# A decoder step's first stage: rope and splitting straight from PSUM, and a weighted sum moved to TensorE

## The chip, the cores and the metric

The kernel runs on one core of a Trainium2 chip. Its engines work side by side, each through its own instruction stream in order: TensorE (PE, with its weight loads shown as PEld), VectorE (DVE), ScalarE (ACT), GpSimd (POOL), and SyncE (SP), whose queue starts nearly all DMA transfers here. The metric is the device time of one execution in microseconds; lower is better. A single run is compared by the median of several executions.

## The reference, cut to what matters

One inference step of a one-layer decoder. 2048 prompt tokens and 32 sample tokens (8 sequences of 4 new tokens) are normed and projected; half of the columns feed a windowed attention of 8 heads of 64, the other half an mLSTM. What matters here is the projection of the attention half, and the sample tokens' attention over a cache of 2048 keys and values per sequence:

```
u = rmsnorm(x) @ w_in;  qa, ka, va, za = columns of u
qa, ka = rope(qa), rope(ka)        # only the first 16 of each head's 64 columns turn:
                                   # x1*cos - x2*sin, x2*cos + x1*sin with x1, x2 = 8 columns each
new_k, new_v = ka, va              # outputs, in float32
# sample tokens, three patterns (window 128, 512, 2048; every key, every 4th, every 16th):
s = einsum('bthe,btjhe->bthj', q, kg) * 64**-0.5
p = exp(s - max);  acc = einsum('bthj,btjhe->bthe', p, vg)   # then merged over the patterns
```

## The kernel before, in words

The program has three stages: `phase_a` (projection, sample attention), `phase_b` (prompt attention), `phase_c` (mLSTM and output). The change is all in `phase_a`. A planner decides the order of the instructions on every engine from its own model of times, except where the program fixes it; then each engine executes its list strictly in order.

`phase_a` first loads the five 1024 x 512 weight blocks (q, k, v and two gates z). Each is scaled by its largest value (`weight_scale`, which needs a `partition_all_reduce` on POOL, L87) and split into a high and a low float16 part, high on ACT, low on DVE (L105) or POOL (L102 and L103). Then it goes over the 16 tiles of 128 prompt tokens. `unit(i, j)` is one tile times one weight block: 24 float16 products of 128 x 128 by 128 x 512 (L143 to L145) into one PSUM bank of four (`ps_proj`, tag "proj").

For q, k and v the unit goes on so: ACT copies the bank to SBUF as float32 `u`, of which there are two buffers (L463); for q and k DVE turns the first 16 columns of every head in `u` with four instructions (L198 to L201); ACT writes the high float16 part to `t16` (L469); POOL subtracts to get the low part (L470); for k ACT copies the high part once more (L472); for v DVE writes two constant columns into `t16` (L474, L475); SP stores `t16` (L476); for k and v POOL scales `u` into `kvout` (L479) and SP stores that to the output (L480). `t16` has one buffer for each of q, k and v, and `kvout` one. For z, ACT copies the bank and SP stores it (L459, L460).

While tiles 4 to 9 run, the loop also prepares six more weight blocks (loaded by L72, written out by L128 from `wst`), and calls `SampleAttention.scores(b)` for the eight sequences: POOL multiplies cached keys by the query (L332), DVE sums (L337). `softmax` follows in tile 9. In tiles 10 to 14 `values(b)` runs for each sequence: for the patterns 2, 1, 0 the cached values (128 keys x 4 tokens x 512, or 128 x 512 shared by the four tokens for pattern 0) are loaded (L317, L321); POOL multiplies patterns 2 and 1 by the probabilities (L382), DVE pattern 0 (L387, four instructions), DVE adds the three (L392, two instructions), and TensorE sums over the keys by one float32 product per token (L395), 32 in all, whose stationary operand is a column of ones in a window of `oh`. The bank `ps_dec` collects all 32 rows. `finish` then divides and stores. The gate units of the last three tiles come after that, and the first products of `phase_b` follow.

Of the kernel before, what the change touches and what calls it, by code (L numbers as in the profile page):

```python
# [10 lines left out]
F32 = mybir.dt.float32  # L11
# [38 lines left out]
def in_order(G, *engines):  # L50
    """Keeps what the block traces on each of these engines in the order of the trace; yields what comes last on each."""
# [14 lines left out]
def weight_loads(G, pool, src, n, tags=("wf", "wf")):  # L66
    """The two halves of src [128, KT, n] (DRAM)."""
# [13 lines left out]
def weight_scale(G, mx, inv, g, rowscale=1.0 / XSC):  # L81
    """The scale of each kt, and inv to undo it, from the four parts' maxima."""
# [25 lines left out]
def weights(G, pool, inv, wf, n, g=None, rowscale=1.0 / XSC, sb=None, dst=None, use=None, shared=0):  # L108
    """wf (of weight_loads) times g, scaled to 2^14 at most, as two float16 parts [128, 2, KT, n], in sb or (DRAM) dst;
    inv undoes the scales. use(j, t) sees the halves t [128, 2, KT / 2, n] that go to dst."""  # L110
# [22 lines left out]
def token_matmuls(nc, ps, x16, tok, hi, lo, cols):  # L133
    """ps[token, col] = x16[:, hi|lo, kt, tok]^T @ (hi|lo)[:, kt, cols], three float16 products."""
    for _ in token_steps(nc, ps, x16, tok, hi, lo, cols):
        pass
# [12 lines left out]
def add_eighths(eng, sq, other):  # L149
    """sq[:, 0] <- the sum of all of sq and other, [128, 4, n] each."""  # L150
# [5 lines left out]
def norm_factors(G, ps, sq, n, tag="", eng=None):  # L156
    """From the squares' sums sq[:, 0] [128, n] the columns' factors, on all partitions: ps[:, 256:256 + n]."""
# [12 lines left out]
def norm_columns(G, pool, pp, xf, x16, n, other, tag="", eng=None):  # L170
    """x16 [128, 2, KT, n] <- rmsnorm (no gain) of the columns of xf [128, KT, n], times XSC, as two float16 parts."""
# [16 lines left out]
def as_f32(x16):  # L188
    """The memory of x16's second part, as [128, 4, 256] float32."""
    return x16[:, 1].rearrange("p k t -> p (k t)").bitcast(F32).rearrange("p (k t) -> p k t", k=4)  # L190


def rope(nc, pool, u, rc, rs, n):
    """u [n, heads, 64] in place; rc, rs [n, 16]."""
# [9 lines left out]
def sample_matmuls(nc, ps, xd, hi, lo, cols):  # L204
    """ps[hi | lo rows of the sample tokens, col]: the two halves are added by the caller."""
# [6 lines left out]
def sample_sum(G, pool, out, ps, sc, n, tag="dhalf"):  # L212
    """out [32, n] = sc * (ps[0:32] + ps[32:64])."""
# [9 lines left out]
def bulk(G, n, after):  # L223
    """The next n pieces of the caches' copies, issued behind an instruction of GpSimd's."""
# [6 lines left out]
class SampleAttention:  # L231
    """Attention of the sample tokens over the cache and the new rows, in steps that the caller spreads out."""

    def __init__(self, G, I, O, pool, pp):
# [5 lines left out]
        self.oh = t("d_oh", [P, 2 * NS])  # L240
        nc.gpsimd.memset(self.oh, 0.0)
        nc.gpsimd.memset(self.oh[:, NS - 1:NS], 1.0)
# [9 lines left out]
    def project(self, j, hi, lo):  # L252
        """j: q, k, v, attention gate, mLSTM gate."""
# [1412 lines left out]
```

## Time and profile before

| | us |
|---|---|
| three runs | 1835.0 (median), 1827.64, 7943.17 |
| span of the profiled execution | 1837.1 |
| PE busy in that span | 1514.6 (82%) |
| DVE busy | 1213.3 (66%) |
| POOL busy | 679.0 (37%) |
| ACT busy | 637.9 (35%) |

The runs' times are those of whole executions; the profile gives for its execution the span from the first to the last instruction and no other time. The profiled span is 2.1 us, or 0.1%, above the median of the runs. Busy time counts an engine's instructions from start to end, and idle time says nothing by itself: what counts is who waits for whom.

### The profile page before, as it was taken

Reading aid. Unit: us, or ns where it says so; the run is one execution under the profiler, and the core shown is the slowest. Engines: PE = TensorE matmul, PEld = TensorE weight load, DVE = VectorE, ACT = ScalarE, POOL = GpSimd, SP = SyncE. Lnnn points to the kernel's source line nnn. Section 1 sums busy time; section 2 is a strip of 40 time slices with the busy share of each in tenths; the row PEclk is TensorE's granted clock in tenths of the full one; section 3 lists DMA queues with packets and bytes.
Section 4 is the critical chain, followed back from the end, with each engine's and each line's share of the span. In section 5 each row is a group of like instructions: output and inputs, shape, how many; then the busy total and the mean of one; then the engine's idle time right before and its main releaser. Section 6 shows DMA issues by size and latency. Waiting matters only on the chain.

```text
span 1837.1 us, 27998 instructions
## 1 busy us (share of the span) xinstructions
PE 1514.6 (82%) x10303; PEld 898.6 (49%) x10303; DVE 1213.3 (66%) x3177; ACT 637.9 (35%) x1330; POOL 679.0 (37%) x836
## 2 busy tenths in 40 slices
PE   2847479777778668999999999688969979898987
PEld 1313234333333222477777886455545545565643
DVE  4541377666677999476766675577668666767765
ACT  2232123123232111276656675233223323232332
POOL 2343045353454788063433677211122212122210
PEclk9978789888979789899989999889989989999998
DMA  5421447676675456396655665635454434446413
GB/s 174 148 93 53 155 142 257 227 274 219 220 245 170 140 162 222 115 333 201 171 201 154 230 217 179 188 99 180 132 159 140 161 128 160 149 163 199 106 41 63
DMA packets 165927, 311.08 MB, mean 169 GB/s; under 512 B 12109, under 2 KB 117742, under 8 KB 155726
## 3 DMA queue, kind: packets, MB, share of 16 engines
q1 hardware_dynamic: 161694, 230.29, 40.9%
q0 software_dynamic: 3952, 78.75, 11.3%
q8 instruction: 81, 1.33, 0.3%
q14 instruction: 56, 0.46, 0.1%
q10 hardware_dynamic: 144, 0.26, 0.0%
HBM read 232.00 MB, written 144.38 MB: 205 GB/s over the span
## 4 chain that ended last, share of the span: by engine, by line
PE 28%; DVE 16%; DMA 10%; issue 4%; ACT 4%; POOL 1%; SPq 0%; POOLq 0%; ACTq 0%; DVEq 0%
DMA Mb<-g_scr 4%; PE ps_s L999 4%; PE ps_t L1021 4%; PE ps_s L1000 4%; DMA A<-att_scr 4%; DVE cd L1156 3%; DVE d_vb L387 2%; PE ps_out L145 2%; PE ps_out L143 2%; PE ps_out L144 2%; PE ps_k L666 1%; PE ps_o L1037 1%; PE ps_o L1038 1%; PE ps_o L1039 1%; PE ps_qk L1140 1%
## 5 line engine op out<-in xcount | busy, mean ns | idle before, releaser
L143 PE MATMUL ps_proj<-wa,x 128*128 128x512 f16 x640 | 253.4, 398 | 37.5 <-ACT u L463 22.6
L144 PE MATMUL ps_proj<-wa,x 128*128 128x512 f16 x640 | 252.8, 397 | 19.4 <-POOL wa L103 19.2
L145 PE MATMUL ps_proj<-wa,x 128*128 128x512 f16 x640 | 252.5, 395 | 0.0
L1008 DVE CUSTOM_DVE_ANT_0 sc<-ps_s,mask,ncqk 128x256 f32<-128x256 f32 (+1 forms) x384 | 144.2, 422 | 53.2 <-PE ps_s L1000 41.8
L1010 POOL TENSOR_SCALAR sc<-sc,o 128x256 f32<-128x256 f32 (+1 forms) x272 | 114.0, 431 | 153.5 <-DVE o L1008 145.1
L144 PEld LDWEIGHTS <-x 128*128 128x128 f16 x768 | 74.6, 100 | 111.8 <-issue 44.8
L1025 DVE SCALAR_TENSOR_TENSOR tl<-ps_t,th 128x512 f16<-128x512 f32 (+1 forms) x152 | 103.1, 681 | 36.5 <-ACT th L1024 35.6
L145 PEld LDWEIGHTS <-x 128*128 128x128 f16 x768 | 75.1, 101 | 104.4 <-issue 36.8
L143 PEld LDWEIGHTS <-x 128*128 128x128 f16 x768 | 75.4, 101 | 103.0 <-issue 27.3
L1024 ACT ACTIVATE th<-ps_t 128x512 f16<-128x512 f32 (+1 forms) x152 | 89.8, 591 | 80.1 <-PE ps_t L1021 78.0
L470 POOL TENSOR_TENSOR t<-u,t 128x512 f16<-128x512 f32 x48 | 67.0, 1397 | 119.1 <-ACT t L469 59.6
L469 ACT ACTIVATE t<-u 128x512 f16<-128x512 f32 x48 | 30.1, 629 | 211.0 <-DVE u L201 107.1
L1021 PE MATMUL ps_t<-c_id,pr 128*128 128x128 f32 x600 | 100.3, 289 | 1.4 <-DVE tl L1025 1.2
L143 PE MATMUL ps_out<-wo,yt 128*128 128x512 f16 x256 | 101.2, 395 | 0.0
L144 PE MATMUL ps_out<-wo,yt 128*128 128x512 f16 x256 | 101.0, 394 | 0.0
L1140 PE MATMUL ps_qk<-cx,wb 128*128 128x256 f16 x256 | 75.1, 293 | 31.0 <-ACT pre L1149 20.7
L145 PE MATMUL ps_out<-wo,yt 128*128 128x512 f16 x256 | 97.3, 390 | 2.9 <-DVE yt L1251 2.9
L1323 POOL TENSOR_TENSOR qi<-qi,qk 128x128 f32<-128x128 f32 x60 | 27.8, 494 | 189.2 <-DMA qi<-g_scr 175.6
L1140 PE MATMUL ps_qk<-early_x,wb 128*128 128x256 f16 x256 | 72.6, 284 | 22.9 <-ACT pre L1149 17.5
L1141 PEld LDWEIGHTS <-wb 128*128 128x128 f16 x512 | 52.8, 103 | 65.2 <-issue 56.2
L1156 DVE SCALAR_TENSOR_TENSOR cd<-pre,cw,cd 128x256 f32<-128x256 f32 x168 | 84.1, 505 | 0.6
L1037 PE MATMUL ps_o<-v,th 128*128 128x65 f16 x600 | 80.4, 196 | 1.5 <-ACT th L1024 1.0
(461 smaller groups left out, 4245.9 us busy)
## 6 DMA issues: line engine op xcount, KB each, us to landing
s_win_k<-cache_win_k POOLq DMA_DIRECT2D x32, 1022.0 KB, 9.3
s_win_v<-cache_win_v POOLq DMA_DIRECT2D x32, 1022.0 KB, 8.0
wf<-w_in SPq DMA_DIRECT2D x18, 1024.0 KB
d_kv<-cache_win_k SPq DMA_DIRECT2D x16, 1024.0 KB
d_kv<-cache_win_v SPq DMA_DIRECT2D x16, 1024.0 KB
A<-att_scr SPq DMA_DIRECT2D x16, 792.0 KB
v<-v_scr SPq DMA_DIRECT2D x12, 1040.0 KB
w_scr<-wst SPq DMA_DIRECT2D x12, 1024.0 KB
```

The costliest lines, as they stand in the source:

```text
L143: nc.tensor.matmul(ps, lhsT=xh, rhs=hi[:, kt, cols], start=kt == 0, stop=False)
L144: nc.tensor.matmul(ps, lhsT=xh, rhs=lo[:, kt, cols], start=False, stop=False)
L145: nc.tensor.matmul(ps, lhsT=xl, rhs=hi[:, kt, cols], start=False, stop=kt == KT - 1)
L999: nc.tensor.matmul(o, lhsT=q, rhs=k[0], start=True, stop=False)
L1008: nc.vector.tensor_tensor_reduce(sc[:, x:x + n], sp[:, x:x + n], G.mask[:, 2 * P - n:], G.ncqk, BIG, ALU.add, ALU.min, nm)
L1010: nc.gpsimd.tensor_scalar(sc[:, x:x + n], sc[:, x:x + n], -1.0, nm, ALU.mult, ALU.add)
L1021: nc.tensor.transpose(out=tp[:, c * P:(c + 1) * P], in_=pr[:, c * P:(c + 1) * P], identity=G.idf)
L1024: nc.scalar.activation(th[:, :w], tp[:, :w], AF.Copy, scale=PSC)
L1025: nc.vector.scalar_tensor_tensor(tl[:, :w], tp[:, :w], PSC, th[:, :w], ALU.mult, ALU.subtract)
L1037: nc.tensor.matmul(o, lhsT=th[:, cs], rhs=V[:, 0:65], start=first, stop=False)
L1140: nc.tensor.matmul(ps, lhsT=hi[:, kt, cols], rhs=x16[:, 0, kt], start=kt == 0, stop=False)
L1156: eng.scalar_tensor_tensor(d, pre[:, j:j + 256], cw[:, ct, j:j + 1], d, ALU.mult, ALU.add)
```

## The change

In `unit`, `u` goes away: ACT and DVE read the PSUM bank directly. The rope table is scaled by 2^-19 on the host, so that its products need no scaling. For q and k DVE forms the two products of rope from the bank (`ra`, and `rb` in one instruction that reads the two halves of 8 columns in reversed order), adds them into a small tile `r`; ACT writes the high part of columns 16 to 63 of every head, and for k and v the scaled float32 output `o`, both from the bank; DVE forms the low part from the bank and the high part with one instruction. POOL only copies and subtracts the 16 turned columns (128 columns in all), and for k scales them into `o`. For v nothing is left on POOL. `t16` of q and k now shares three buffers; v has two of its own, whose constant columns are set once; `o` has two.

In `values` the multiplication by probabilities and the sum over keys become one float32 product per pattern and token: its stationary operand is the 128 x 32 block of probabilities (4 tokens x 8 heads) and its moving operand the 128 x 512 values. The four tokens' products go to four different groups of 32 partitions of one bank (tag "den", one buffer) and accumulate over the three patterns. DVE then keeps of every row the head that belongs to it (a mask), and one more float32 product with a 0/1 matrix adds the 128 rows into the 32 rows of `ps_dec`. Mask and matrix come in one small constant, `c_dsel`, by a DMA that takes the place of two memsets on POOL.

```diff
-        self.oh = t("d_oh", [P, 2 * NS])
-        nc.gpsimd.memset(self.oh, 0.0)
-        nc.gpsimd.memset(self.oh[:, NS - 1:NS], 1.0)
+        self.sel = t("d_sel", [P, HA + 2 * NS - NTOK])
+        nc.sync.dma_start(out=self.sel, in_=I["c_dsel"])
...
-        acc = None
+        ps = self.pp.tile([P, 512], F32, tag="den", name="ps_dv", bufs=1)
         for a in (2, 1, 0):
-            p = self.sc[:, a, b].rearrange("p t h -> p (t h)").unsqueeze(2).broadcast_to([P, NTOK * HA, DA])
             t = self.piece("cache_win_v", b, a, ("wst", "wf", "d_kv")[a])
-            tv = t.rearrange("p t (h d) -> p (t h) d", d=DA)
-            if a:
-                nc.gpsimd.tensor_tensor(tv, tv, p, ALU.mult)
-            else:
-                u = self.pool.tile([P, NTOK, 512], F32, tag="d_qb", name="d_vb")
-                for i in range(NTOK):
-                    pi = self.sc[:, 0, b, i].unsqueeze(2).broadcast_to([P, HA, DA])
-                    nc.vector.tensor_tensor(u[:, i].rearrange("p (h d) -> p h d", d=DA), t[:, 0].rearrange("p (h d) -> p h d", d=DA), pi, ALU.mult)
-                t = u
-            if acc is None:
-                acc = t
-            else:
-                nc.vector.tensor_tensor(acc, acc, t, ALU.add)
-        for i in range(NTOK):
-            r = b * NTOK + i
-            nc.tensor.matmul(self.ps_o[:NS], lhsT=self.oh[:, NS - 1 - r:2 * NS - 1 - r], rhs=acc[:, i], start=r == 0, stop=r == NS - 1)
+            p = self.sc[:, a, b].rearrange("p t h -> p (t h)")
+            for i in range(NTOK):
+                nc.tensor.matmul(ps[i * 32:(i + 1) * 32], lhsT=p, rhs=t[:, i if a else 0], start=a == 2, stop=a == 0)
+        u = self.pool.tile([P, HA, DA], F32, tag="d_z", name="d_vs")
+        nc.vector.tensor_tensor(u, ps.rearrange("p (h d) -> p h d", d=DA), self.sel[:, 0:HA].unsqueeze(2).broadcast_to([P, HA, DA]), ALU.mult)
+        c0 = HA + NS - NTOK - b * NTOK
+        nc.tensor.matmul(self.ps_o[:NS], lhsT=self.sel[:, c0:c0 + NS], rhs=u.rearrange("p h d -> p (h d)"), start=b == 0, stop=b == NB - 1)
...
+        v16 = [pool.tile([P, HA, 130], F16, tag=f"v16{j}", name="v16") for j in range(2)]
+        for t in v16:
+            nc.gpsimd.memset(t[:, :, 64:65], 1.0)
+            nc.gpsimd.memset(t[:, :, 65:66], 0.0)
...
-            u = pool.tile([P, 512], F32, tag="u", name="u", bufs=2)
-            nc.scalar.activation(u, ps, AF.Copy, scale=USC)
-            uh = u.rearrange("p (h d) -> p h d", d=DA)
+            pv = ps.rearrange("p (h d) -> p h d", d=DA)
+            R = 0 if j == 2 else 16
+            t16 = v16[i % 2] if j == 2 else pool.tile([P, HA, (2 * DA, 3 * DA)[j]], F16, tag="t16", name="t16", bufs=3)
+            l0 = 66 if j == 2 else DA
+            o = pool.tile([P, HA, DA], F32, tag="kvout", name="kvout", bufs=2) if j else None
             if j < 2:
-                rope(nc, pool, uh, G.rope_p[:, i, 0:16], G.rope_p[:, i, 16:32], P)
-            w, l0, scr = ((2 * DA, DA, G.q_scr), (3 * DA, DA, G.k_scr), (130, 66, G.v_scr))[j]
-            t16 = pool.tile([P, HA, w], F16, tag=f"t16{j}", name="t16")
-            nc.scalar.activation(t16[:, :, 0:DA], uh, AF.Copy)
-            nc.gpsimd.tensor_tensor(t16[:, :, l0:l0 + DA], uh, t16[:, :, 0:DA], ALU.subtract)
+                ra = pool.tile([P, HA, 16], F32, tag="ra", name="ra")
+                rb = pool.tile([P, HA, 16], F32, tag="rb", name="rb")
+                r = pool.tile([P, HA, 16], F32, tag="rr", name="rr", bufs=2)
+                table = lambda c, n: G.rope_p[:, i, c:c + n].unsqueeze(1).broadcast_to([P, HA, n])
+                nc.vector.tensor_tensor(ra, pv[:, :, 0:16], table(0, 16), ALU.mult)
+                two = lambda x: x.rearrange("p h (a e) -> p h a e", a=2)
+                nc.vector.tensor_tensor(two(rb), two(pv[:, :, 0:16])[:, :, ::-1], two(table(16, 16)), ALU.mult)
+            nc.scalar.activation(t16[:, :, R:DA], pv[:, :, R:], AF.Copy, scale=USC)
+            if j:
+                nc.scalar.activation(o[:, :, R:], pv[:, :, R:], AF.Copy, scale=G.wainv[:, j:j + 1])
+            nc.vector.scalar_tensor_tensor(t16[:, :, l0 + R:l0 + DA], pv[:, :, R:], USC, t16[:, :, R:DA], ALU.mult, ALU.subtract)
+            if j < 2:
+                nc.vector.tensor_tensor(r, ra, rb, ALU.add)
+                nc.gpsimd.tensor_copy(t16[:, :, 0:16], r)
+                nc.gpsimd.tensor_tensor(t16[:, :, DA:DA + 16], r, t16[:, :, 0:16], ALU.subtract)
             if j == 1:
+                nc.gpsimd.tensor_scalar(o[:, :, 0:16], r, G.isc[:, 1:2], 0.0, ALU.mult, ALU.add)
                 nc.scalar.activation(t16[:, :, 2 * DA:], t16[:, :, 0:DA], AF.Copy)
-            elif j == 2:
-                nc.vector.memset(t16[:, :, 64:65], 1.0)
-                nc.vector.memset(t16[:, :, 65:66], 0.0)
...
-                nc.gpsimd.tensor_scalar(o, u, G.isc[:, j:j + 1], 0.0, ALU.mult, ALU.add)
```

## Rows read from the trace of the kernel before

**Rows 1.** The stages: busy us of each engine, granted clock, DMA share, GB/s.

```profile
0.00:196.00 196.00, 117.15 (x520) 51.17 (x521) 79.77 (x189) 54.75 (x94) 67.86 (x100) 0.90 0.40 127
196.00:300.00 104.00, 70.70 (x372) 32.95 (x372) 63.20 (x96) 26.20 (x37) 36.59 (x17) 0.84 0.48 153
300.00:590.00 290.00, 232.01 (x1137) 103.35 (x1135) 197.01 (x259) 79.96 (x122) 129.63 (x64) 0.89 0.69 234
590.00:736.00 146.00, 100.27 (x442) 37.74 (x443) 137.57 (x103) 20.26 (x34) 115.81 (x40) 0.84 0.53 170
```

**Rows 2.** PE's waits from 0 to 300: who, us in total, times, longest.

```profile
PE ps_proj L143 <- ACT u L463: 18.7, 3, 9.3
...
PE ps_ss L162 <- DVE sq L153: 29.6, 2, 20.2
PE ps_proj L143 <- ACT z L459: 4.2, 1, 4.2
```

**Rows 3.** What ACT's copy of the bank (L463) waited for; POOL's all-reduce.

```profile
  POOL t L470: 52.1, 14
...
L87 POOLq MODIFY_POOL_CONFIG  x24: 1/11/37, 24.6 to 496.5; - x24
```

**Rows 4.** POOL, SP, DVE and PE around 210, in order of time.

```profile
204.23 1.11 POOL L470 TENSOR_TENSOR t<-u,t 128x512 f16<-128x512 f32 x1 [7.45 <-issue]
...
208.98 0.07 DVE L474 MEMSET t<- 128x8 f16 x1 [8.49 <-DMA v_scr<-t]
210.45 0.59 SPq L72 DMA_DIRECT2D wf<-w_in  x1
218.60 2.35 DVE L78 TENSOR_REDUCE wmx<-wf 128x1 f32<-128x1024 f32 x2 [8.59 <-DMA wf<-w_in]
223.32 1.01 PE L162 MATMUL ps_ss<-ones,sq 128*128 128x1 f32 x4 [20.23 <-DVE sq L153]
```

**Rows 5.** POOL's groups from 300 to 600; SP's longest waits from 0 to 800.

```profile
L470 POOL TENSOR_TENSOR t<-u,t 128x512 f16<-128x512 f32 x22 | 26.0, 1180 | 66.6 <-ACT t L469 36.6 <-issue 23.2 <-ACT x L176 6.9
L479 POOL TENSOR_SCALAR kvout<-u,isc 128x512 f32<-128x512 f32 x14 | 12.1, 861 | 24.6 <-DVE u L201 14.9 <-DVE t L475 7.7 <-issue 2.0
...
SPq L476 <- POOL t L470: 164.8, 35, 17.8
SPq L480 <- POOL kvout L479: 82.5, 21, 17.3
```

**Rows 6.** Groups of the values' stretch, 590 to 736: busy us, mean ns, idle before.

```profile
L382 POOL TENSOR_TENSOR d_kv<-d_kv,d_sc 128x2048 f32<-128x2048 f32 x16 | 64.2, 4025 | 7.0 <-DMA d_kv<-cache_win_v 6.2 <-ACT d_sc L352 0.8
L387 DVE TENSOR_TENSOR d_vb<-d_kv,d_sc 128x512 f32<-128x512 f32 x32 | 60.6, 1949 | 0.0
L395 PE MATMUL ps_dec<-d_kv,d_oh 128*32 128x512 f32 x56 | 30.9, 704 | 20.8 <-DVE d_kv L392 20.8
L392 DVE TENSOR_TENSOR d_kv<-d_kv 128x2048 f32<-128x2048 f32 x8 | 20.1, 2514 | 0.0
```

**Rows 7.** DVE instructions by line: ns min/median/max, first and last start.

```profile
L198 DVE TENSOR_TENSOR ra<-u,rope_p x32: 272/291/4406, 52.8 to 714.2; 128x128 f32<-128x128 f32 x32
L1025 DVE SCALAR_TENSOR_TENSOR tl<-ps_t,th x152: 543/689/693, 780.8 to 1129.7; 128x512 f16<-128x512 f32 x144, 128x384 f16<-128x384 f32 x8
L404 DVE TENSOR_TENSOR d_rep<-d_rep,ps_dec x1: 650/650/650, 745.4 to 745.4; 32x512 f32<-32x512 f32 x1
```

**Rows 8.** Weight loads of the values' float32 products (two for each product), in order.

```profile
738.29 0.18 PEld L395 LDWEIGHTS ps_dec<-d_kv,d_oh 128*32 128x32 f32 x1 [0.68 <-issue]
...
740.74 0.11 PEld L395 LDWEIGHTS ps_dec<-d_kv,d_oh 128*32 128x32 f32 x1 [0.32 <-issue]
```

**Rows 9.** POOL and ACT instructions nearest to the new ones; waits for DVE's rope.

```profile
L841 POOL COPY dT<-dT 128x192 f32<-128x192 f32 x1 | 0.4, 393 | 0.0
L857 POOL TENSOR_TENSOR dT<-dT 128x128 f32<-128x128 f32 x1 | 0.5, 460 | 0.0
...
  ACT t L469: 107.1, 13
```

More of the change, by code (lines that the diff above doesn't have):

```diff
@@ L471, in unit @@
             if j == 1:
+                nc.gpsimd.tensor_scalar(o[:, :, 0:16], r, G.isc[:, 1:2], 0.0, ALU.mult, ALU.add)
                 nc.scalar.activation(t16[:, :, 2 * DA:], t16[:, :, 0:DA], AF.Copy)
-            elif j == 2:
-                nc.vector.memset(t16[:, :, 64:65], 1.0)
-                nc.vector.memset(t16[:, :, 65:66], 0.0)
+            scr = (G.q_scr, G.k_scr, G.v_scr)[j]
             nc.sync.dma_start(out=scr.rearrange("r t e -> t r e")[rows], in_=t16.rearrange("p (r h) e -> p r (h e)", r=4))
@@ L477, in unit @@
             if j:
-                o = pool.tile([P, 512], F32, tag="kvout", name="kvout")
-                nc.gpsimd.tensor_scalar(o, u, G.isc[:, j:j + 1], 0.0, ALU.mult, ALU.add)
-                nc.sync.dma_start(out=O["p_win_k" if j == 1 else "p_win_v"][rows, :], in_=o)
+                nc.sync.dma_start(out=O["p_win_k" if j == 1 else "p_win_v"][rows, :], in_=o.rearrange("p h d -> p (h d)"))
         def gate_unit(i):
@@ L1575, in constants @@
 def constants():
-    rp = _rope_table(np.arange(S)).reshape(NT, P, 32).transpose(1, 0, 2)
+    rp = _rope_table(np.arange(S)).reshape(NT, P, 32).transpose(1, 0, 2) * np.float32(USC)
     t = np.arange(P)
@@ L1583, in constants @@
     dmask = np.where(key < np.arange(NTOK)[None, :], -BIG, 0.0).astype(np.float32)
+    i, i2, h = np.arange(P) // 32, np.arange(P) // HA % NTOK, np.arange(P) % HA
+    keep = (i == i2)[:, None] & (h[:, None] == np.arange(HA)[None, :])
+    dsel = np.concatenate([keep, np.arange(2 * NS - NTOK)[None, :] == (NS - NTOK + i)[:, None]], axis=1).astype(np.float32)
     r = np.arange(NS)
@@ L1590, in constants @@
     rs = _rope_table(16384 + r % NTOK)
-    return {"c_dmask": dmask, "c_d32": d32, "c_block": block, "c_rope_s": rs, "c_causal": causal, "c_rope_p": rp, "c_mask": mask, "c_id": np.eye(P, dtype=np.float32)}
+    return {"c_dsel": dsel, "c_dmask": dmask, "c_d32": d32, "c_block": block, "c_rope_s": rs, "c_causal": causal, "c_rope_p": rp, "c_mask": mask, "c_id": np.eye(P, dtype=np.float32)}
 def host_layout(a):
```

## The prediction, made before the change was run

> **What bounds the kernel now.** I first read the stages [rows 1]. Up to 736 us no engine is full for long: PE is busy 117.2 of 196 us, 70.7 of 104, 232.0 of 290 and 100.3 of 146. After 770 the kernel is a different one, and the change touches nothing there. So the question is what makes PE wait in the first 770 us, and that has a different answer in each stretch. In the views of waits one looks for what the waiting instruction waited for, and then for what that one waited for, until an engine is reached that was really working.
>
> Before 300 us the waits [rows 2] name ACT's copy of the bank (18.7 us), ACT's copy of a gate (4.2 us) and a DVE sum (29.6 us, of which 20.2 in one piece). ACT's copy in turn mostly waited for POOL's subtraction L470, 52.1 us over the program [rows 3]: there are two buffers `u`, and POOL gives them back. POOL is not busy but it stands still: each of the twelve all-reduces L87 comes with two changes of its configuration (24 in rows 3), and around one of them one sees the first ordinary instruction behind a gap of 7.45 us [rows 4]. Whatever is queued on POOL pays for these gaps.
>
> From 300 to 590 PE is ahead of everything else, and the slow thing is the chain load, largest value, all-reduce, split, store of each weight block, beside the scores, on POOL, DVE and SP. SP issues in order and waits 164.8 us for L470's results and 82.5 us for `kvout`, and the loads behind these wait with them [rows 5].
>
> From 590 to 736 DVE is the bound: 137.6 of 146 us [rows 1]. Of that L387 is 60.6 us and L392 20.1 us twice (the row shown and its twin, 40 us), together 101 us; POOL's L382 is another 64.2 us, and PE waits 20.8 us for the sum [rows 6]. Much of L387 is not work: its mean is 1949 ns, while the rope instruction L198, also from SBUF and SBUF, takes 291 ns in the median and 4406 at most [rows 7]; the long ones lie beside POOL's long multiplications.
>
> **The change part by part.** *Evacuation, 0 to 196 us.* What goes: PE's 18.7 us behind `u` and 4.2 us behind the gate [rows 2], 22.9 us in all, since a bank no longer needs a buffer that POOL gives back. What is next: the weight blocks still come at the pace of POOL's all-reduces, which stay with their gaps, and this pace may eat all of it. Bounds 0 and 22.9 us; I take 10, a little under half, because in this stretch PE's work already waits for weights as well.
>
> *The constant columns, 196 to 223 us.* Here one can follow a chain by eye [rows 4]: POOL comes late to L470 (204.23, after its gap), v's tile is stored after it, DVE's memset L474 waits for that store because v has a single buffer (8.49 us), behind it on DVE stands the last split of a weight, behind that the load of the next weights (210.45), and PE finally stands still until 223.32. The memsets leave the loop and v has two buffers, so DVE's 8.49 us go. I take 8.5, bounds 0 and 8.5: the load must then still land.
>
> *POOL in the loop, 300 to 590 us.* Out go L470 and L479, 26.0 and 12.1 us [rows 5], that is 38.1 us for 22 units, 7.3 tiles. In come, per tile, for q a copy and a subtraction of 128 columns, bounded by 393 and 460 ns [rows 9], 0.85 us; for k the same and one scaling, at most 0.39 us more, 1.24 us; for v nothing. 7.3 x 2.1 = 15 us. POOL saves 23 us; with SP's queue less often behind POOL I take 12 as what reaches the end, bounds 0 (DVE, or a transfer, is late instead) and 23.
>
> What DVE and ACT get: DVE loses two of its eight rope instructions per tile and the memsets, and gets three low parts, priced by L1025 (bank and SBUF, 543 ns for 384 columns at least, 689 for 512): 0.54 + 0.54 + 0.69 = 1.8 us per tile. Against that, only the sum `ra + rb` still reads two SBUF tiles. L1025 works from a bank while POOL is also busy, and never took more than 693 ns in 152 [rows 7], so I cost DVE at nothing net; if DVE is on the path there, it is up to 7.3 x 1.8 = 13 us, which lies inside the bounds above. ACT's waits for DVE's rope (107.1 us, [rows 9]) lose their reason, but a new one stands in their place: k's second copy now waits for POOL's copy of 16 columns, and behind it on ACT are the next banks and the weights' high parts. ACT stood at the same place before, for DVE, so I add nothing for this. A bank is now held until DVE has read it too; with four banks PE may run four units ahead.
>
> *The values, 590 to 736 us.* DVE loses 101 us and gets eight maskings of a bank at 650 ns (L404, [rows 7]), 5 us. It falls to 137.6 - 101 + 5 = 42 us, POOL loses 64.2 us. Next late is PE or the transfers. PE now has 100.3 us of which 30.9 are L395, so 69.4 of other work. The new float32 products are 8 x (12 + 1) = 104 where 32 were. One product is two weight loads and two passes, and a pass takes 0.11 + 0.32 = 0.43 us late in the group and 0.18 + 0.68 = 0.86 us early [rows 8], that is at the 2.4 and at the 1.2 GHz level; PE had waited before the early ones. No row shows products to four different groups of 32 partitions, so their overlap is bounded from both sides. None: 104 x 0.86 = 89 us at 2.4 GHz. Full, four for one: 8 x (3 + 1) x 0.86 = 27.5 us. I take the value between them that follows from order: PE takes instructions in order, the two passes of one product use the same columns and must follow each other, but the second pass of one can run beside the first of the next. Four products then take five passes, and the stretch 8 x (3 x 5 x 0.43 + 0.86) = 58 us. PE's sum is 69.4 + 58 = 127.5 us against 146: 18.5 us gained. Each sequence's products also wait for DVE to have masked the bank of the one before (one buffer), 0.65 us, with other units to put between. The transfers: 170 GB/s over 146 us are 24.8 MB [rows 1]; at the 234 GB/s of the stretch before they need 106 us, so they bound the gain at 40.
>
> The Trainium skill speaks to this term (TensorEngine Tiling (Array Packing), Key Properties): different tiles of the array run their loads and products in parallel, and changing the tiling drains the engine. No row of this trace shows the first; by it all four products would run at once, and the third rival below is what that gives. The second speaks against the change, since the units' 128-column products stand between; L395 already mixes 32-column products with them, so the old kernel pays it too.
>
> *The small constant* is one transfer for two memsets on POOL at the first stage's start, and hidden there.
>
> The sum: 10 + 8.5 + 12 + 18.5 = 49 us. The profiled span is 0.1% above the median of the runs, so it comes off the median: 1835 - 49 = 1786 us.
>
> **The rivals.** *Products one after the other.* If groups of 32 columns don't overlap at all, and at the mean of this trace (30.9 us for 28 products, 1.10 us each), the 104 take 115 us and PE 184 us, 38 more than the stretch has now. 1835 - 30.5 + 38 = 1843 us. For it: no row shows an overlap. Against: PE is ahead of the stretch when it begins and could have done more of the units earlier.
>
> *Products at the 1.2 GHz level: the slower side.* The products now wait in PE's order for each loaded piece, 24 of them, with the units queued behind. If PE stands still before each as it did before L395, the products begin at the lower level: 104 x 2 x 0.86 = 179 us without overlap, PE 248 us, 102 more than now: 1835 - 30.5 + 102 = 1907 us. It decides once a product costs PE more than (146 + 30.5 - 69.4) / 104 = 1.03 us, and is slower by over 2% from 1.4 us. For it: the early loads of rows 8 and the granted clock of 0.84 in that stretch, one of the two lowest. Against: fewer engines have to meet before a product can start.
>
> *Full overlap.* PE needs 69.4 + 27.5 = 97 us, the transfers 106: gain 40 us, 1835 - 30.5 - 40 = 1764 us. For it: the groups share no columns. Against: the two passes of each product.
>
> *The change doesn't reach the path:* POOL's gaps and the loads hold the first 590 us as before, and only the values' 18.5 us come: 1816 us. For it: 0.40 to 0.69 DMA share and the all-reduces stay. Against: the chain of rows 4 and SP's waits both start at what is removed.
>
> **How the numbers follow.** Forecast 1786 us (own range 1762 to 1812): 0.42. Full overlap: 0.18. One after the other: 0.17. Not on the path: 0.10. The lower level: 0.13. Below every bound: 22.9 + 8.5 + 23 + 40 = 94 us gain, 1741 us. The range 1741 to 1843 leaves out the slower rival and little else. A measurement of this kernel tells about 2% from no change, so faster is below 1798 us: 0.18 and three quarters of 0.42 and a few of the others, 0.53. Slower, above 1872 us: 0.13 and a little for an order that the planner gets wrong, 0.15. The rest, 0.32, is the same.
>
> **What would show it.** Right: no waits of PE on ACT's copy; DVE's waits for v's store gone and the 20 us gap before 223 halved; SP's waits for POOL's results under a third; DVE below half in the values' stretch, and that stretch 15 to 40 us shorter; the second product of a group starting before the first ends. Wrong: PE waiting for DVE to free a bank, ACT waiting for POOL's copy for tens of us, the values' products in a row at 0.86 us each with the units late behind them, or a first stage that ends where it did, with the loads as the reason.

## The result, and the profile after

The changed kernel takes 1744.2 us (median) beside 1828.5 us for the kernel before; the ratio is 0.953 with a 95% interval of 0.949 to 0.957. It is faster by 84 us where 49 were forecast. Executions more than 1.5% above the fastest of their kernel, such as the one of 7943 us before, are left out of all medians and ratios.

Both programs can be cut at the same four points, and the first rows to read are those that place them. This is one line of each kernel, with its durations in ns (min/median/max) and its first and last start: first, in the kernel before, the softmax's exponential, and then the products of scores in `phase_b`.

```profile
L352 ACT ACTIVATE d_sc<-d_sc x1: 835/835/835, 592.2 to 592.2; 128x768 f32<-128x768 f32 x1
L999 PE MATMUL ps_s<-qn x192: 218/394/445, 768.8 to 1083.9; 128*128 128x256 f16 x108, 128*128 128x128 f16 x84
```

The same two lines in the changed kernel:

```profile
L351 ACT ACTIVATE d_sc<-d_sc x1: 842/842/842, 560.0 to 560.0; 128x768 f32<-128x768 f32 x1
L1003 PE MATMUL ps_s<-qn x192: 218/392/446, 692.8 to 1005.1; 128*128 128x256 f16 x108, 128*128 128x128 f16 x84
```

The exponential comes 32.2 us earlier, the first scores of the second stage 76.0 us earlier. A third point is the product at which PE stood still for 20.23 us at 223.32 us [rows 4]. In the changed kernel it starts at 199.53 us, and the number in brackets, the idle time before it, is 10.98. The timeline of PE there, with the other pauses of more than 2.4 us from 75 us on:

```profile
78.42 0.61 PE L143 MATMUL ps_proj<-wa,x 128*128 128x512 f16 x1 [4.41 <-DVE t L473]
...
105.36 0.39 PE L143 MATMUL ps_proj<-wa,x 128*128 128x512 f16 x1 [4.54 <-DVE t L473]
...
119.09 0.61 PE L143 MATMUL ps_proj<-wa,x 128*128 128x512 f16 x1 [7.76 <-DVE t L473]
...
126.75 0.59 PE L144 MATMUL ps_proj<-wa,x 128*128 128x512 f16 x1 [5.77 <-POOL wa L103]
...
136.27 0.39 PE L143 MATMUL ps_proj<-wa,x 128*128 128x512 f16 x1 [2.47 <-DVE t L473]
...
199.53 1.01 PE L162 MATMUL ps_ss<-ones,sq 128*128 128x1 f32 x4 [10.98 <-DVE sq L153]
```

The kernel before, its pauses of PE of more than 1 us in the same part; the last one is the 20.23 us of [rows 4]:

```profile
98.67 0.59 PE L143 MATMUL ps_proj<-wa,x 128*128 128x512 f16 x1 [7.55 <-ACT u L463]
...
103.03 0.38 PE L144 MATMUL ps_proj<-wa,x 128*128 128x512 f16 x1 [1.32 <-POOL wa L103]
...
123.01 0.59 PE L144 MATMUL ps_proj<-wa,x 128*128 128x512 f16 x1 [15.69 <-POOL wa L103]
...
150.87 0.58 PE L143 MATMUL ps_proj<-wa,x 128*128 128x512 f16 x1 [9.33 <-ACT u L463]
...
160.60 0.38 PE L143 MATMUL ps_proj<-wa,x 128*128 128x512 f16 x1 [1.84 <-ACT u L463]
...
197.27 0.58 PE L143 MATMUL ps_proj<-wa,x 128*128 128x512 f16 x1 [4.22 <-ACT z L459]
```

No product waits for ACT's copy of a bank any more, but four wait for DVE's low part, 19.2 us. That is almost what was removed there (18.7 + 4.2 us, [rows 2]). It still paid, because of where the waits lie. From 75 to 127 us little changes: the kernel before pauses for 24.6 us (7.55, 1.32 and 15.69), the changed one for 22.5 us (three of the new waits, 16.7 us, and 5.77 for POOL's part of a weight). Behind that the kernel before pauses for 9.33, 1.84, 4.22 and 20.23 us, the changed one only for 2.47 and 10.98. These 22 us are nearly all of the 23.8 us by which the product comes earlier.

The stages of the changed kernel: each engine's busy us with its number of instructions, then granted clock, DMA share, GB/s. The cuts are the product at 200, the softmax and the first scores.

```profile
core 0: us, PE busy (x) PEld busy (x) DVE busy (x) ACT busy (x) POOL busy (x), PEclk, DMA share, GB/s
0.00:200.00 200.00, 120.92 (x535) 52.79 (x535) 93.52 (x204) 57.35 (x100) 58.96 (x104) 0.88 0.44 142
200.00:560.00 360.00, 298.79 (x1499) 133.16 (x1499) 235.51 (x325) 93.37 (x144) 148.43 (x82) 0.91 0.67 225
560.00:693.00 133.00, 125.33 (x756) 50.80 (x757) 38.54 (x109) 24.08 (x46) 16.02 (x21) 0.96 0.58 196
```

One reads the third row against [rows 1]: where DVE was busy for 137.6 of 146 us, it now is for 38.5 of 133, and PE for 125.3 of 133. The bound has moved from DVE to PE. The groups of the values' products in their own stretch, 560 to 651 us (busy us, mean ns, idle before):

```profile
L382 PE MATMUL ps_dv<-d_kv,d_sc 128*32 128x512 f32 x192 | 29.3, 600 | 0.0
...
L386 PE MATMUL ps_dec<-d_vs,d_sel 128*32 128x512 f32 x16 | 8.4, 604 | 0.0
...
L384 DVE TENSOR_TENSOR d_vs<-ps_dv,d_sel 128x512 f32<-128x512 f32 x8 | 5.5, 688 | 16.4 <-PE ps_dv L382 16.4
```

192 passes, two for each of 96 products, would take 82.6 us in a row at 0.43 us from one to the next [rows 8]; the mean duration of 600 ns is longer than that distance, so it can't be added up. The group is busy for 29.3 us. Most passes therefore run beside others. The timeline shows how, for the first sequence: start, duration, and x for the merged count.

```profile
575.65 0.16 PEld L382 LDWEIGHTS ps_dv<-d_kv,d_sc 128*32 128x32 f32 x8 [0.42 <-issue]
575.65 2.78 PE L382 MATMUL ps_dv<-d_kv,d_sc 128*32 128x512 f32 x24
576.11 0.13 PEld L382 LDWEIGHTS ps_dv<-d_kv,d_sc 128*32 128x32 f32 x4 [0.30 <-issue]
576.54 0.13 PEld L382 LDWEIGHTS ps_dv<-d_kv,d_sc 128*32 128x32 f32 x4 [0.30 <-issue]
```

Every 0.43 us four weight loads come together, one for each group of 32 partitions, and with them four passes: 24 passes take 2.78 us, little more than six times 0.43.

### The profile page after: what moved, and what is told of

The parts are those of the page before. It is cut to its first block, busy times and chain, and to the rows that moved or that the text cites. A ratio compares the mean times of both kernels' runs of the same rounds, so it can differ in the third digit from the quotient of the medians.

```text
span 1742.3 us, 28167 instructions
## 1 busy us (share of the span) xinstructions
PE 1492.9 (86%) x10447; PEld 888.9 (51%) x10447; DVE 1090.7 (63%) x3121; ACT 621.9 (36%) x1314; POOL 549.9 (32%) x822
## 4 chain that ended last, share of the span: by engine, by line
PE 34%; DVE 18%; DMA 14%; issue 6%; ACT 4%; POOL 3%; SPq 0%; POOLq 0%; ACTq 0%; DVEq 0%
DMA A<-att_scr 4%; PE ps_s L1003 4%; PE ps_t L1025 4%; PE ps_s L1004 4%; DMA Mb<-g_scr 4%; DVE cd L1160 3%; PE ps_proj L143 2%; PE ps_proj L145 2%; PE ps_proj L144 2%; PE ps_out L145 2%; PE ps_out L143 2%; PE ps_out L144 2%; DVE wst L105 2%; DMA d_qb<-ds_scr 2%; PE ps_k L670 1%
## 5 line engine op out<-in xcount | busy, mean ns | idle before, releaser
L143 PE MATMUL ps_proj<-wa,x 128*128 128x512 f16 x640 | 253.1, 397 | 34.4 <-DVE t L473 23.7
L143 PE MATMUL ps_out<-wo,yt 128*128 128x512 f16 x256 | 99.4, 388 | 0.0
L144 PE MATMUL ps_out<-wo,yt 128*128 128x512 f16 x256 | 98.9, 386 | 0.0
L145 PE MATMUL ps_out<-wo,yt 128*128 128x512 f16 x256 | 95.5, 383 | 3.9 <-DVE yt L1255 3.9
L331 POOL TENSOR_TENSOR d_kv<-d_kv,d_qb 128x2048 f32<-128x2048 f32 x16 | 74.9, 4701 | 25.5 <-DMA d_kv<-cache_win_k 13.6
L1042 PE MATMUL ps_o<-v,th 128*128 128x64 f16 x600 | 78.6, 195 | 0.0
```

What stands on the lines that cost most here:

```text
L143: nc.tensor.matmul(ps, lhsT=xh, rhs=hi[:, kt, cols], start=kt == 0, stop=False)
L144: nc.tensor.matmul(ps, lhsT=xh, rhs=lo[:, kt, cols], start=False, stop=False)
L145: nc.tensor.matmul(ps, lhsT=xl, rhs=hi[:, kt, cols], start=False, stop=kt == KT - 1)
L1042: nc.tensor.matmul(o[:, 0:64], lhsT=th[:, cs], rhs=V[:, 66:130], start=False, stop=False)
```

## The experiments

Four times of each kernel's profiled execution make the results comparable: the product that stood at 223 us, the softmax, the first scores of `phase_b`, and the span. The last two columns are the median of its runs and the ratio to the kernel before, run beside it, with its interval.

| kernel | product | softmax | scores | span | median | ratio |
|---|---|---|---|---|---|---|
| before | 223.3 | 592.2 | 768.8 | 1837.1 | 1828.5 | |
| before, again | 221.6 | 592.3 | 768.0 | 1827.3 | 1829.2 | |
| after | 199.5 | 560.0 | 692.8 | 1742.3 | 1744.2 | 0.953 (0.949-0.957) |
| 1 values alone | 223.4 | 592.5 | 725.2 | 1780.7 | 1782.8 | 0.978 (0.972-0.984) |
| 2 units alone | 200.2 | 559.4 | 722.1 | 1780.0 | 1783.5 | 0.977 (0.974-0.981) |
| 3 one group of columns | 198.0 | 558.5 | 731.4 | 1787.4 | 1789.2 | 0.980 (0.976-0.984) |
| 4 v's tile twice | 214.6 | 582.7 | 757.1 | 1820.5 | 1822.7 | 0.998 (0.995-1.001) |
| 5 four buffers u | 211.8 | 571.8 | 755.4 | 1823.7 | 1822.6 | 0.996 (0.992-0.999) |
| 6 u and v's tile | 212.9 | 572.6 | 757.7 | 1811.7 | 1822.6 | 0.996 (0.992-1.000) |
| 7 POOL's load, free | 221.7 | 587.8 | 715.7 | 1764.6 | 1766.6 | 0.966 (0.960-0.972) |
| 8 POOL's load in the unit | 208.9 | 584.6 | 711.5 | 1756.6 | 1763.4 | 0.967 (0.963-0.971) |
| 9 after, scores on DVE | 200.7 | 534.3 | 672.1 | 1726.9 | 1721.5 | 0.940 (0.935-0.945) |
| 10 as 9, norms on DVE | 199.2 | 547.2 | 678.2 | 1735.6 | 1736.8 | 0.951 (0.948-0.955) |
| 11 before, scores on DVE | 222.3 | 569.4 | 745.9 | 1800.1 | 1804.4 | 0.990 (0.982-0.998) |

**1, the values alone.** The kernel before with the new `values`, `c_dsel` and the rest of that half of the diff.

> The kernel before with the new sum of values alone; the units, their copies and stores are the old ones. Theory (two gains that add): the stretch from the softmax to the first scores of the second stage shortens by the 44 us that it shortened in the changed kernel, the softmax stays near 592 us, and the time is 1831.8 - 44 = 1788 us (1778 to 1798). Rival (the units' load on DVE and POOL has to go as well, since they stand in the same stretch): under 25 us come, over 1807 us. Rival (the values give everything): 1744 to 1760 us.

The softmax is at 592.5 us as before, and from there to the scores it takes 132.7 us: 43.9 less than before, and the same 132.8 as in the changed kernel. The first theory holds. The units' old work on DVE and POOL, which still stands in this stretch, costs nothing there any more: DVE is busy for 30.8 of 133 us and PE for 127.6.

```profile
592.00:725.00 133.00, 127.57 (x769) 52.37 (x770) 30.75 (x110) 29.55 (x52) 27.97 (x24) 0.97 0.58 199
```

**2, the units alone.** The changed kernel with the old `values` and `oh`.

> The changed kernel with the old sum of values on POOL and DVE. Theory (two gains that add): the softmax comes near 560 us as in the changed kernel, the stretch behind it stays near 176 us, and the time is 1831.8 - 32 - (up to 12 more from the stretch behind) = 1788 to 1800 us. Rival (the units do not reach the path): over 1815 us. Rival (the old values get in the way of the new units, because DVE is the bound there): 1800 to 1815 us with the softmax at 560.

The softmax is at 559.4 us, the changed kernel's time, and the stretch behind it shrinks by 13.9 us to 162.7: part of the lighter load on DVE and POOL does reach the old values. The time, 1783.5 us, lies 4.5 us below what was expected, away from both rivals. So the two halves almost add. Up to the scores the values give 43.6, the units 46.7, and both together 76.0, because those 14 us lie in the stretch that the new values shorten by themselves.

**3, one group of columns.**

```diff
-                nc.tensor.matmul(ps[i * 32:(i + 1) * 32], lhsT=p, rhs=t[:, i if a else 0], start=a == 2, stop=a == 0)
+                g = 0 if a else i
+                nc.tensor.matmul(ps[g * 32:(g + 1) * 32], lhsT=p, rhs=t[:, i if a else 0], start=(a == 2 and i == 0) or (a == 0 and i > 0), stop=a == 0)
```

> The changed kernel, but the products of patterns 2 and 1 of all four tokens go to the same 32 columns (the output lacks these patterns for three tokens of four; the sums of the first token are mixed); counts, operands and waits are unchanged. Theory (the four groups of columns run at the same time, and PE is the bound there): 64 of the 96 products no longer overlap, 16 groups take 3.44 us instead of 0.86, PE needs 41 us more from 560 to 651 us, and the time is 1744 + 41 = 1785 us (1772 to 1790). Rival (transfers are the bound there, PE has room): under 15 us more, below 1760 us. Rival (the groups did not overlap in the first place): 1744 us.

The time rises by 45 us. The timeline's first group, and the group of all products from 558 to 731 us:

```profile
573.80 7.91 PE L383 MATMUL ps_dv<-d_kv,d_sc 128*32 128x512 f32 x24
```

```profile
L383 PE MATMUL ps_dv<-d_kv,d_sc 128*32 128x512 f32 x192 | 63.6, 596 | 0.0
```

The same 24 passes take 7.91 us instead of 2.78, and all of them 63.6 us instead of 29.3. The softmax to the scores takes 172.9 us, 40.1 more. The overlap of the four groups is shown, it is worth some 40 us, and PE has no room to hide its loss; the transfers are not the bound.

**4, v's tile twice**, in the kernel before.

```diff
+        v16 = [pool.tile([P, HA, 130], F16, tag=f"v16{j}", name="v16") for j in range(2)]
+        for t in v16:
+            nc.gpsimd.memset(t[:, :, 64:65], 1.0)
+            nc.gpsimd.memset(t[:, :, 65:66], 0.0)
...
-            t16 = pool.tile([P, HA, w], F16, tag=f"t16{j}", name="t16")
+            t16 = v16[i % 2] if j == 2 else pool.tile([P, HA, w], F16, tag=f"t16{j}", name="t16")
...
-            elif j == 2:
-                nc.vector.memset(t16[:, :, 64:65], 1.0)
-                nc.vector.memset(t16[:, :, 65:66], 0.0)
```

> The kernel before with v's float16 tile in two buffers whose constant columns are set once, and nothing else. Theory by the prediction's second step: DVE's wait of 8.49 us for v's store goes, and PE's standstill before 223 us halves: 1831.8 - 8.5 = 1823 us. Rival (the weight load behind it has other late parents): the standstill stays near 20 us and the time within 2 us of 1831.8. Rival (this one wait is most of the unit's gain): below 1810 us.

The product comes 8.7 us earlier, the softmax 9.5 us. The wait before the product has shrunk from 20.23 to 13.23 us, by a third where a half was expected:

```profile
214.62 1.01 PE L162 MATMUL ps_ss<-ones,sq 128*128 128x1 f32 x4 [13.23 <-DVE sq L153]
```

In the whole time the gain is 4.4 us with an interval from 10 us to none, so there it is not told apart from zero; at its place it is the 8.5 us that were forecast.

**5, four buffers for u**, in the kernel before.

```diff
-            u = pool.tile([P, 512], F32, tag="u", name="u", bufs=2)
+            u = pool.tile([P, 512], F32, tag="u", name="u", bufs=4)
```

> The kernel before with four buffers for u instead of two, and nothing else: ACT can empty all four banks before POOL has given one u back. Theory (the units' gain before 200 us comes from PE no longer waiting for a buffer that POOL holds): PE's waits for ACT's copy fall from 18.7 us to under 5, the products that stood at 223 us begin 10 us or more earlier, and the time is 1827 - 10 = 1817 us. Rival (POOL's pace and the store of v behind it still decide; more buffers only lengthen the queue): the products at 223 us move by less than 3 us, and the time stays within 4 us of 1827.

The product moves by 11.5 us and the softmax by 20.4. PE's waits for ACT's copy fall to 8.7 us, not under 5. Some 8 us come at the end: the old values take 7 us longer behind the softmax, where DVE is the bound.

**6, both together**, with three buffers u and not the four of run 5, so that it is not exactly the sum of runs 4 and 5.

> The kernel before with three buffers u and v's tile twice with its constant columns set once; POOL's work is the old one. Theory (before 220 us the gain is one of buffers: 8.7 us by v's tile and 11.5 us by u, each alone, at the products that stood at 223 us): the two add, these products begin at 201 to 206 us, the softmax at 565 to 572 us, the time is 1812 to 1820 us, since the old values keep DVE as the bound behind the softmax. Rival (both remove the same standstill): 210 to 213 us and 1820 to 1826 us.

The rival is right: the product is at 212.9 us and the softmax at 572.6. Each of the two alone nearly does the same: they remove one standstill, as far as three buffers can stand for four. With POOL's old work in place, more buffers stop at 212 us, while the changed kernel is at 199.5.

**7, POOL's load put back on a tile of its own**, in the changed kernel (`pad` is 64 partitions that no other instruction reads).

```diff
+            nc.gpsimd.tensor_tensor(pad[:, 1], pad[:, 0], pad[:, 0], ALU.subtract)
+            if j:
+                nc.gpsimd.tensor_scalar(pad[:, 1], pad[:, 0], G.isc[64:128, j:j + 1], 0.0, ALU.mult, ALU.add)
```

> The changed kernel, in which POOL does the removed amount of work once more on a tile that nobody else reads: per unit of q, k, v a subtraction of 512 columns, for k and v a scaling of 512 columns too, some 38 us from 300 to 590 us. Theory (POOL's time was on the path, so that its relief paid the loop's 8 us and part of what came before 200): 8 to 25 us more, 1752 to 1769 us. Rival (what paid was that banks, stores and the next weights no longer depend on POOL; its time itself is free): under 5 us more, and the softmax within 4 us of 560.

It costs 22 us, and 27.8 at the softmax. But since the load waits for nothing, it was ordered early: 50.0 us of it ran before 240 us, where the old kernel had 20 before 223. How much the old place costs can't be read from this, so the next run ties it to the unit.

**8, the load in its old place**: as 7, but both instructions read the unit's `t16[64:128, :, 0:64]`.

> The changed kernel with the removed work of POOL once more, now reading the unit's own float16 tile, so that it stands where the old work stood (the load of the run before depended on nothing, and 50 us of it ran before 240 us where the old kernel had 20). Theory (POOL's time was on the path): the softmax at 570 to 585 us, 1754 to 1769 us. Rival (its time was free, what paid was that banks and stores no longer wait for POOL): the softmax within 4 us of 560, under 5 us more.

The product comes 9.4 us later than in the changed kernel and the softmax 24.6 us, and the kernel takes 19 us more. At the product that need not be POOL's time alone, because the load also holds the unit's tile until POOL has read it: ACT waits for it before it can write v's high part, and PE waits for ACT next.

```profile
174.93 0.60 ACT L473 ACTIVATE v<-ps_proj 128x512 f16<-128x512 f32 x1 [15.11 <-POOL d_u L488]
...
176.73 0.59 PE L143 MATMUL ps_proj<-wa,x 128*128 128x512 f16 x1 [11.24 <-ACT z L457]
```

From the product to the softmax no wait of ACT for the load is left, and there it adds 15.2 us (375.7 against 360.5): in the loop POOL's work was on the path, whether by its time in the queue or by holding up DVE.

**9, the scores' products on DVE**, in the changed kernel.

```diff
-                nc.gpsimd.tensor_tensor(t, t, qb, ALU.mult)
+                nc.vector.tensor_tensor(t, t, qb, ALU.mult)
```

> The changed kernel with the sixteen multiplications of cached keys on DVE instead of POOL (4.5 to 5.9 us each there; by the same size on DVE 2.28 us each, 36.5 us together). Theory (a long instruction of POOL holds up DVE's instructions that read two SBUF tiles): the 0.2 to 0.4 us instructions of DVE that took over 4 us between 238 and 548 us take their normal time, PE's 55 us of waits for the norms' sums fall to under 40, and the time falls by 5 to 15 us to 1730 to 1740. Rival (DVE is then the late one): 36 us more of DVE in 235 to 548 us, PE waits longer for the norms, 1750 to 1770 us.

This beats both kernels: 1721.5 us, 8.5 us below what was expected; its interval and that of the changed kernel don't meet, and the softmax comes 25.7 us earlier. Three lines of the changed kernel and then the same three here show why it was tried: an addition of 32 x 8 numbers, POOL's or DVE's multiplication, and the rope's sum.

```profile
L754 DVE TENSOR_TENSOR gates_s<-gates_s,gbias x1: 4445/4445/4445, 239.5 to 239.5; 32x8 f32<-32x8 f32 x1
L331 POOL TENSOR_TENSOR d_kv<-d_kv,d_qb x16: 4497/4530/5891, 238.0 to 533.0; 128x2048 f32<-128x2048 f32 x16
L475 DVE TENSOR_TENSOR rr<-ra,rb x32: 270/292/4084, 55.1 to 650.7; 128x128 f32<-128x128 f32 x32
```

```profile
L754 DVE TENSOR_TENSOR gates_s<-gates_s,gbias x1: 147/147/147, 241.0 to 241.0; 32x8 f32<-32x8 f32 x1
L331 DVE TENSOR_TENSOR d_kv<-d_kv,d_qb x16: 2274/2285/6157, 241.1 to 509.3; 128x2048 f32<-128x2048 f32 x16
L475 DVE TENSOR_TENSOR rr<-ra,rb x32: 268/284/3875, 55.6 to 631.0; 128x128 f32<-128x128 f32 x32
```

The addition falls from 4445 to 147 ns. PE's waits for the norms' sums fall from 55.0 to 34.6 us. The stretched instructions are not gone (3875 at most), since the norms still run on POOL.

**10, the norms' long instructions on DVE too.**

```diff
-            norm_columns(G, pool, pp, xf, x16, 256, as_f32(x16), eng=nc.gpsimd)
+            norm_columns(G, pool, pp, xf, x16, 256, as_f32(x16))
```

> The run with the scores' products on DVE, and in it the two long instructions of each of six norms on DVE too (POOL 4.6 and 4.2 us each, 53 us together; by DVE's time for the same columns 2.28 us each, 27 us). Theory (a long instruction of POOL costs DVE more than the same work on DVE itself): 3 to 12 us less than 1721.5, 1710 to 1718 us. Rival (DVE, which has taken 36 us already, is then late for the weights and the scores): 1725 to 1740 us.

The rival is right: 15 us slower than run 9. The two instructions take 2.29 us each on DVE, as expected, but PE now waits 20.6 us for the norms' factors (5.0 in run 9). Its waits for the norms' sums fell from 34.6 to 22.8 us at the same time, so these waits explain the loss only in part. Relief of POOL paid here only as long as DVE was not the later one.

**11, the scores' products on DVE in the kernel before.**

> The kernel before with the sixteen multiplications of cached keys on DVE, as the run that made the changed kernel 23 us faster. Theory (a long instruction of POOL holds up DVE and the small work queued on POOL, whatever the units do): the softmax comes 15 to 30 us earlier than 592 us and the time falls by 12 to 30 us, 1802 to 1819 us. Rival (the gain needs DVE's room that only the change made): within 6 us of 1831, or slower.

22.8 us at the softmax, 24 us by the medians, 19 by the ratio (4 to 33): run 9's gain doesn't need the change.

**Before, again**: the unchanged kernel, for its profile.

> The kernel before once more, for a second profile of it. Theory (the change ends with the first stage, and the rest of the difference between the two profiles is scatter between executions): from the first scores of the second stage to the end it takes 1050 to 1060 us instead of 1068. Rival (the changed first stage makes the third stage shorter): 1065 us or more again.

From the first scores to the end it takes 1059.2 us, 9 less than in the first profile of the same kernel.

## Why the prediction was right and where it was short

The sign and the places were right, and the size was short. 1744.2 us lies 18 us below the forecast's own range (1762 to 1812) and only 3 us inside the wide one (1741 to 1843). The steps of the change give 76.0 us; the rest of the way down are 8.3 us in the later stages, which had no term, and 6.5 us because the forecast started from 1835.0 us, where the median is 1828.5. In the table the first and the last measured value are remainders:

| step | forecast (bounds) | measured | where |
|---|---|---|---|
| evacuation | 10 (0 to 22.9) | 15.1 | 23.8 us at the product, less the next row |
| constant columns | 8.5 (0 to 8.5) | 8.7 | run 4, at the product |
| POOL in the loop | 12 (0 to 23) | 8.4 | product to softmax, 368.9 to 360.5 us |
| values | 18.5 (-38 to 40) | 43.8 | softmax to scores, 176.6 to 132.8 us |
| rest of the program | 0 | 8.3 | 84.3 by the medians less 76.0 |

**The units.** 30.5 us were forecast up to the softmax, and 32.2 came, for the reason given: POOL's time and the buffers that it held. That the sum came so near is in part luck, since 5 us too little in the first step and 4 too much in the third cancel. Put back in its place, POOL's work returns 24.6 of the 32.2 us (run 8). That the evacuation and the constant columns are two terms, though, was half wrong: in runs 4 to 6 either cure alone moves the product by 8.7 or 11.5 us and both by 10.4, so they had one standstill in common. What the changed kernel has beyond them, some 12 us more at the product, came with POOL's relief; run 8 takes back 9.4 of it, in part by a tile that its load holds, so how much of the 12 is POOL's time stays open. In the loop the load costs 15.2 us, near the 12 that were forecast for its relief. The mark of the evacuation term was met, no product waits for ACT's copy. But one of the wrong signs was met too: PE now waits 23.7 us, up to the softmax, for DVE's low part to free a bank. The profile after shows why it cost little: 16.7 us of it lie ahead of 127 us, where the kernel before pauses for as long in all, for a buffer and for weights.

**The values: the term that was mis-sized.** The step that failed is the middle value, "four products then take five passes", 58 us on PE. It rested on the idea that the two passes of one product must follow each other in PE's order and so hold up the next product. The traces show the bound that was left for a rival: in order, but with four passes side by side, four products in the time of one. The group took 29.3 us and the eight sums over rows 8.4 us, 37.7 together, against 27.5 for the full overlap and 58 for the middle value; run 3 takes the overlap away for two thirds of the products and pays 40 us. So the forecast of the stretch should have been the rival's 40, which had a chance of 0.18, and 43.8 came. The other part of the step was right: DVE's 101 us were the bound, and eight maskings of 0.69 us took their place.

The transfers, which I had as a cap at 40 us, are not the bound; PE is (125.3 of 133 us). The sum missed this because it stopped at 736 us, where PE still had a full 33 us of work to do before the first scores. These are the rows of the kernel before over the whole stretch, each engine's busy time and then the old values' products:

```profile
592.00:769.00 177.00, 133.27 (x617) 52.42 (x618) 150.91 (x150) 29.03 (x52) 114.52 (x40) 0.86 0.46 149
...
L395 PE MATMUL ps_dec<-d_kv,d_oh 128*32 128x512 f32 x64 | 36.1, 717 | 20.8 <-DVE d_kv L392 20.8
```

By the prediction's own working PE's sum is then 133.3 - 36.1 + 27.5 = 124.7 us, near the 125.3 measured (in part by chance, since the new products took 37.7 and the rest, at a higher granted clock, less), while the transfers, 149 GB/s over 177 us, need 113 us at 234 GB/s: PE ends later, and the cap at 40 falls.

The rival at the 1.2 GHz level didn't come near: the granted clock in this stretch is 0.96, with PE busy for 125.3 of 133 us, where it was 0.84 before [rows 1], with PE busy for 100.3 of 146.

The Trainium skill, TensorEngine Tiling (Array Packing), Key Properties, says that different tiles load weights and multiply in parallel; the trace agrees, also for float32 products in two passes (24 passes in 2.78 us, 7.91 when eight of twelve products share their columns). Its other sentence there, that a change of the tiling drains the engine, has a small price here at most: the units' 128-column products stand between the values' groups, PE is idle for 7.7 of 133 us, and the first 24 passes take 0.2 us more than six rounds of 0.43.

**SP, ACT and DVE.** SP's waits for POOL's results were 164.8 us for the low parts and 82.5 for `kvout` [rows 5], and should fall under a third. The changed kernel's waits of SP up to 700 us, in total, times, longest:

```profile
SPq L484 <- POOL kvout L479: 57.8, 7, 16.4
...
SPq L482 <- POOL t L477: 35.0, 12, 12.2
SPq L482 <- DVE t L473: 33.7, 8, 8.5
...
SPq L482 <- POOL t L476: 15.3, 2, 14.8
```

For POOL's `t` it is 50.3 us, just under a third, with 33.7 for DVE beside it. For `kvout` there are still 57.8 of 82.5 us, so that together 44% are left and the sign was not met: the scaling of 128 columns stands in the same queue behind the same long instructions, and its shortness doesn't help. That may be why the loop's term stayed below the 12 us. ACT's second copy of k waits 52.0 us for POOL's copy of 16 columns, in seven pieces of up to 18.4 us. That was named as a wrong sign and did happen; it cost little, for PE's waits for the weights' parts that stand behind it on ACT (L125) are 12.1 us, where they were 9.8. The other signs of being right were met (the pause before the product is down from 20.23 to 10.98 us, DVE is busy for 38.5 of 133 us behind the softmax), save that this stretch is 43.8 us shorter and not 15 to 40.

**The remaining 8.3 us.** The change ends with the first stage. From the first scores on, DVE's 2483, ACT's 1026 and POOL's 615 instructions stand in the same order in both traces, yet the two profiles take 1068.3 and 1049.5 us for them. Much of that is scatter: the kernel before alone gives 1068.3 and 1059.2. Over all profiles here that part takes from 1045.1 to 1068.3 us, with a mean of 1061 in the six without either half of the change and of 1053 in the eight with one or both; the two sets overlap (1053.9 to 1068.3, and 1045.1 to 1057.9). Whether the shorter first stage really gives 8 us to the rest is left open. Run 9 points to no simple link: it begins the second stage 20.7 us earlier than the changed kernel and takes 5.3 us longer for it.

## What to carry to other kernels

Where a cost is bounded from both sides and the two ends are far apart, a middle value is not the safe one: ask which end the kernel is likely to be at, and give that end its own weight. Add such a sum up to the point where the next stage really begins, or an engine that looks free may turn out to be the bound. An engine that is only a third busy can still set the pace, if it stands in everyone's queue: take its small jobs away from it, or its long ones, and measure at a point in the middle of the program, where a few us can be seen. Two waits for the same late thing can be one gain, not two.

## What the runs showed of the hardware

A long instruction on POOL holds up DVE's short ones, and by more than a sharing of the time in halves would. The timeline of the changed kernel from 238 us, in order of time:

```profile
237.99 5.89 POOL L331 TENSOR_TENSOR d_kv<-d_kv,d_qb 128x2048 f32<-128x2048 f32 x1 [13.65 <-DMA d_kv<-cache_win_k]
...
238.22 0.17 DVE L296 TENSOR_TENSOR d_sn<-d_sn,d_c 32x32 f32<-32x32 f32 x1
238.32 1.20 DVE L151 TENSOR_TENSOR sq<-sq,x 128x1024 f32<-128x1024 f32 x1
...
239.45 4.45 DVE L754 TENSOR_TENSOR gates_s<-gates_s,gbias 32x8 f32<-32x8 f32 x1
243.83 0.27 DVE L475 TENSOR_TENSOR rr<-ra,rb 128x128 f32<-128x128 f32 x1
...
244.15 0.53 DVE L473 SCALAR_TENSOR_TENSOR t<-ps_proj,t 128x384 f16<-128x384 f32 x1
...
244.65 4.99 POOL L331 TENSOR_TENSOR d_kv<-d_kv,d_qb 128x2048 f32<-128x2048 f32 x1
245.31 4.60 DVE L153 TENSOR_TENSOR sq<-sq 128x256 f32<-128x256 f32 x1
```

Two of DVE's short instructions, L754 and L153, start after POOL's long one and end with it, at 243.90 (POOL 243.88) and 249.91 (POOL 249.64) us; both have two inputs in SBUF. Which of two engines goes first can't be read from the start times alone: L296 and L151, which have two such inputs too, also start after POOL's first L331 and take no longer than in run 9 (0.17 and 1.21 us), and it is POOL's instruction that takes 5.89 us instead of its median of 4.53. The new instruction that reads the bank and one tile (L473) never took more than 0.69 us in 48. It goes the other way as well: in run 9, where DVE does the multiplication, POOL's subtraction of 128 columns, 0.47 us in the mean of the changed kernel, takes 2.95 us. It started while DVE's L152 was running, and DVE's L331 came right behind that.

```profile
244.08 0.72 DVE L152 TENSOR_TENSOR sq<-sq 128x512 f32<-128x512 f32 x1
244.34 2.95 POOL L477 TENSOR_TENSOR t<-rr,t 128x128 f16<-128x128 f32 x1
244.73 2.27 DVE L331 TENSOR_TENSOR d_kv<-d_kv,d_qb 128x2048 f32<-128x2048 f32 x1
```

The Trainium skill, SBUF — State Buffer, SBUF: two separate sides, has the rule: DVE instructions with two SBUF inputs and GpSimd instructions that read SBUF share a pair of ports, which one of them holds for its whole instruction while the other waits. Both timelines agree with it in that one engine stands until the other's instruction ends; in the second, DVE's sum, which also has two SBUF inputs, had started first. They don't show that the earlier start in the profile decides, as L296 and L151 above tell. How much of the 23 us of run 9 comes from this hold and how much from POOL's shorter queue was not separated.
